# Attention scores in PSUM tiles of 1024 keys, with two tiles for transposed probabilities

## The chip, the cores and the metric

One core of one Trainium2 chip runs the kernel. The metric is the device time of one execution in microseconds (us), and the number compared is the median of a kernel's runs. Engines are named as the profile names them: PE multiplies matrices (PEld is its weight load, which overlaps PE), DVE is VectorE, ACT is ScalarE, POOL is GpSimd, SP issues DMAs. PE writes its results to PSUM, which has 8 banks of 2 KiB in each of 128 partitions; a bank holds 512 float32 values.

## What is computed

One layer of a decoder. A projection of the normalised input gives queries, keys, values, an indexer's queries and keys, gates, and the inputs of a gated MLP. The indexer chooses at most 256 causal keys for each of 2048 prompt queries; attention runs over the chosen keys only; the two halves are gated, joined, projected and added to the residual. 64 sample queries do the same against paged caches. Cut to the part in question:

```python
def sparse_attend(q, kg, vg, valid):          # 8 query heads x 64, 4 key heads
    s = jnp.einsum('btgrd,btkgd->btgrk', qg, kg) * HEAD_DIM ** -0.5
    s = jnp.where(valid[:, :, None, None, :], s, -jnp.inf)
    p = jax.nn.softmax(s, axis=-1).astype(vg.dtype)
    o = jnp.einsum('btgrk,btkgd->btgrd', p, vg)
```

The kernel doesn't gather: it computes all causal scores and adds a mask that the selection left in memory.

## The kernel before

Three phases follow each other. Phase A projects and selects. Phase B (`phase_b`) is the attention, and the change lies in it alone. Phase C is the output projection and the gate.

Phase B takes the prompt in 16 blocks `i` of 128 queries; block `i` sees `W = 128 * (i + 1)` keys. A block has four steps, one for each key head `g`, and a step has the two query heads `r` that share it. For each step two lists of units are made and interleaved by even spacing:

- `scores(i, g)`: for each head, chunks of 512 keys. A chunk is two matmuls into a PSUM tile `b_s` (a high and a low part of the queries, L1117 and L1118) and one DVE instruction (L1119) which adds the mask, writes the masked scores to `b_sm` in SBUF and keeps the running minimum in `b_st`; each chunk but the first takes the minimum of the one before as its start, and a short read of the accumulator follows each. After the last chunk ACT takes the exponential of the whole row in place (L1126).
- `values(i, g)` of the step before: pairs of key blocks. A pair is four PE transposes of probabilities into one PSUM tile `b_tp` (L1152), a split into `b_pt` by the helper at L126 and L127 (ACT copies the high part, then DVE subtracts it from the tile to get the low part, so the tile is held until DVE has read it), and, two pairs later, one matmul for each key block with the values into `b_o` (L1169). At the end of a step ACT and DVE add the two halves of `b_o` (L1185, L1186 to `b_x`), two PE transposes turn it (L1193), and POOL scales it.

Between units, `sample_attention` is drawn on as a filler: it transposes cache pages into `b_tp` tiles too (L1318, copied by ACT at L1320), takes `b_s` tiles for its scores (L1327, L1330) and `b_tp` tiles for its outputs (L1373). `prep_q` transposes the next block's queries through `b_tp` (L1050).

PSUM in phase B is four `b_tp` tiles of a bank, two `b_s` tiles of a bank and two `b_o` tiles of a bank, which is all eight. The pools hand tiles out in rotation, so a new tile waits for the last reader of the one that had its place. The program's scheduler decides the final order on each engine; each engine then runs its list in that order.

Of the kernel before, what the change touches and what calls it, by code (L numbers as in the profile page):

```python
# [9 lines left out]
F32 = mybir.dt.float32  # L10
# [7 lines left out]
PSUM = bass.MemoryType.PSUM  # L18
# [28 lines left out]
SPS = 0  # L47
SY = 8
X_POOL = 0
SPB = 2  # L50
# [63 lines left out]
class Builder:  # L114
# [961 lines left out]
    def phase_b(self, eb):  # L1076
        tc, nc, I, O = self.tc, self.nc, self.I, self.O
# [6 lines left out]
        with ExitStack() as es:  # L1084
            pool = lambda name, bufs, **kw: es.enter_context(tc.tile_pool(name=name, bufs=bufs, reuse_waits="tile", **kw))
# [1 line left out]
            smp = pool("b_sm", LAG_SM)  # L1087
            ptp = pool("b_pt", 2 + PV_LAG)
            wk = pool("b_wk", 2)
            tp = pool("b_tp", 6 - SPB - SPS, space=PSUM)  # L1090
            sps = pool("b_sps", SPS, space=PSUM) if SPS else tp
            sp = pool("b_s", SPB, space=PSUM)
            op = pool("b_o", 2, space=PSUM)
            Kst, Vst, ms, prs = self.Kst, self.Vst, self.ms, self.prs
# [3 lines left out]
            def scores(i, g, pr):  # L1098
                qh, ql, ga, stt = pr
                m = ms[i]  # L1100
                W = 128 * (i + 1)
                out, units = [], []
                for r in range(2):
                    h = 2 * g + r
                    if W > SEQ // 2:
                        sm = smp.tile([128, SEQ], F32, name="b_sm")[:, :W]
                    else:
                        if r == 0:
                            both = smp.tile([128, 2, SEQ // 2], F32, name="b_sm")
                        sm = both[:, r, :W]  # L1110
                    out.append(sm)

                    def chunk(c, h=h, sm=sm):
                        c0, cn = c * 512, min(512, W - c * 512)
                        ps = sp.tile([128, 512], F32, name="b_s")[:, :cn]
                        rhs = Kst[c][:, g, :cn]
                        nc.tensor.matmul(ps, lhsT=qh[:, h], rhs=rhs, start=True, stop=False)  # L1117
                        nc.tensor.matmul(ps, lhsT=ql[:, h], rhs=rhs, start=False, stop=True)  # L1118
                        V.tensor_tensor_reduce(out=sm[:, c0:c0 + cn], in0=ps, in1=m[:, c0:c0 + cn], scale=1.0,  # L1119
                                               scalar=3.0e38 if c == 0 else stt[:, h, c - 1:c], op0=OP.add, op1=OP.min,  # L1120
                                               accum_out=stt[:, h, c:c + 1])

                    def expo(e, h=h, sm=sm):
                        part = sm[:, e * EXP:min(W, e * EXP + EXP)]
                        c = -(-W // 512) - 1
                        nc.scalar.activation(part, part, AF.Exp, bias=stt[:, h, c:c + 1], scale=-1.0,  # L1126
                                             accum_out=stt[:, h, 4 + e:5 + e])
                        if e:
                            V.tensor_tensor(stt[:, h, 4:5], stt[:, h, 4:5], stt[:, h, 5:6], OP.add)

                    ne = -(-W // EXP)
                    units += [(lambda c=c, f=chunk: f(c)) for c in range(-(-W // 512) - 1)]
                    units += [lambda f=chunk, e=expo: (f(-(-W // 512) - 1), e(0))]
                    if ne > 1:
                        units += [lambda e=expo: e(1)]
                sms[i, g] = out
                return units
# [70 lines left out]
            sms, obs, tail = {}, {}, []  # L1208
            fill = self.sample_attention(sc, sp, sps)
            fill_n = 0.0  # L1210
            parts = lambda b: 2 * -(-(b + 1) // 4) + -(-(b + 1) // 2) + 1
            rate = FILL / (sum(4 * parts(b) for b in ORDER) - FILL_AT * parts(ORDER[0]))
            due = []
            for si in range(len(steps) + max(LAG, LAG_SMALL)):
                A, B = [], []
                if si < len(steps):
                    i, g = steps[si]
                    A = scores(i, g, prs[i])
                    at = si // 4
                    if g == 1 and at + 2 < NB:  # L1220
                        self.load_mask(ORDER[at + 2])
                    due.append((si + (LAG_SMALL if i < 7 else LAG), steps[si]))
# [28 lines left out]
    def sample_attention(self, c, sp, tp):  # L1251
        tc, nc, I, O = self.tc, self.nc, self.I, self.O
# [16 lines left out]
        ps = tp.tile([128, 2, 2, 128], F32, name="b_tp")  # L1269
# [10 lines left out]
        ps = tp.tile([128, 2, 2, 128], F32, name="b_tp")  # L1280
# [11 lines left out]
        def fetch():  # L1292
            if todo:
                s, ch = todo.pop(0)
                pg = c.tile([128, 2, 256], F32, name="s_pg", bufs=6)
                self.pages(pg.rearrange("p k d -> p (k d)"), "cache_k", s, ch, 2)
                pgs.append(pg)

        fetch()
        for hf in range(2):  # L1300
# [6 lines left out]
            for ch in range(5):  # L1307
                n = 256 if ch < 4 else 64
                kTs = {}
                for s4 in range(4):  # L1310
                    s = hf * 4 + s4
                    if ch < 4:
                        pg = pgs.pop(0)
                        fetch()
                        for p in range(2):
                            ps = tp.tile([128, 2, 2, 128], F32, name="b_tp").rearrange("p a b n -> p (a b n)")
                            for k in range(2):
                                nc.tensor.transpose(ps[:, k * 128:k * 128 + 128], pg[:, k, p * 128:p * 128 + 128], ident)  # L1318
                            kT = c.tile([128, 256], F32, name="s_kT", bufs=8)
                            nc.scalar.activation(kT.rearrange("d (x k) -> d x k", k=2), ps[:, :256].rearrange("d (k x) -> d x k", k=2), AF.Copy)  # L1320
                            kTs[s4, p] = kT
                            yield
                for p in range(2):
                    S = sp.tile([128, 512], F32, name="b_s")[:, :n]
                    for s4 in range(4):
                        kT = kTs[s4, p] if ch < 4 else knT[:, p]
                        nc.tensor.matmul(S[s4 * 32:s4 * 32 + 32], lhsT=QS[:, hf * 4 + s4, p].rearrange("p g r t -> p (g r t)"),  # L1327
                                         rhs=kT, start=True, stop=True, tile_position=(0, s4 * 32))
                    w = stt[:, hf * 2 + p]
                    V.tensor_tensor_reduce(out=SM[p][:, ch * 256:ch * 256 + n], in0=S,  # L1330
                                           in1=m[:, ch * 256:ch * 256 + n], scale=1.0,
                                           scalar=3.0e38 if ch == 0 else w[:, ch - 1:ch], op0=OP.add, op1=OP.min,
                                           accum_out=w[:, ch:ch + 1])
                    yield
# [16 lines left out]
            for kb in range(9):  # L1351
                kr = 128 if kb < 8 else 64
                ps = tp.tile([128, 2, 2, 128], F32, name="b_tp")
# [11 lines left out]
            for ch in range(5):  # L1365
                kbs = range(2 * ch, min(9, 2 * ch + 2))
                o = tp.tile([128, 2, 2, 128], F32, name="b_tp")
                for kb in kbs:
                    kr = 128 if kb < 8 else 64
                    for p in range(2):  # L1370
                        for s4 in range(4):
                            vt = vts[ch, s4][:, kb % 2] if kb < 8 else vn
                            nc.tensor.matmul(o[s4 * 32:s4 * 32 + 32, p, 0], lhsT=pts[kb][:kr, p, s4 * 32:s4 * 32 + 32],  # L1373
                                             rhs=vt[:kr, p * 128:p * 128 + 128], start=(kb == kbs[0] and p == 0),
                                             stop=(kb == kbs[-1]), tile_position=(0, s4 * 32), skip_group_check=True)
# [8 lines left out]
            ps = tp.tile([128, 2, 2, 128], F32, name="b_tp")  # L1384
# [9 lines left out]
        ps = tp.tile([128, 2, 2, 128], F32, name="b_tp")  # L1394
# [206 lines left out]
```

## Time and profile before

| | |
|---|---|
| median of 3 runs | 1873.06 us (1872.78 to 1878.46) |
| profiled execution: its own time | 1874.53 us |
| its span, first to last instruction | 1872.7 us |
| around the span | 1.8 us |
| phase B | 1026 to 1515 us, 489 us |
| busy over the span: PE, DVE, ACT, POOL | 97%, 66%, 54%, 32% |

Busy time is the union of instruction durations. PE's durations overlap, so its share alone doesn't tell how much room it has; the distance between the starts of neighbouring matmuls does. A chain of waits follows the last instruction back to what released it. Idle time on an engine that nobody waits for costs nothing.

### The profile page before, as it was taken

How to read it: one execution, taken by the hardware profiler on the slowest of the kernel's cores; microseconds unless marked ns; L12 is line 12 of the kernel's file. 1: busy time of each engine (PE TensorE's matmuls, PEld its weight loads, DVE VectorE, ACT ScalarE, POOL GpSimd, SP SyncE). 2: the span in 40 equal slices, each digit the busy share in tenths (PEclk: the TensorE clock that was granted, in tenths of full speed). 3: DMA queues.
4: the chain of work that ended last, by engine and by line, in shares of the span. 5: the costliest groups of instructions: out<-in, count | busy, mean ns of one | idle time of the engine just before them, and what ended most of it. 6: DMA issues, size and time to landing. Idle time of an engine off the chain costs nothing. (4 is left out here: it accounts for less than half of the span.)

```text
span 1872.7 us, 33926 instructions
## 1 busy us (share of the span) xinstructions
PE 1821.9 (97%) x11974; PEld 1599.1 (85%) x11974; DVE 1243.2 (66%) x3638; ACT 1019.7 (54%) x1912; POOL 608.2 (32%) x967
## 2 busy tenths in 40 slices
PE   7998999999999999999999899999999999999998
PEld 6997978999999999998988777788778878888887
DVE  4588753568788638768754788899979974233321
ACT  3234434446656636677665888688867753122121
POOL 4566362433013325004403642522234113222221
PEclk9998999999999999999999899999999999999999
DMA  8854665645445564454455551522133063223211
GB/s 241 283 182 145 212 204 188 212 126 157 127 154 167 201 185 144 142 169 154 151 195 169 144 138 49 157 63 72 54 87 116 12 226 109 75 96 107 93 37 46
DMA packets 243807, 261.54 MB, mean 140 GB/s; under 512 B 83177, under 2 KB 209841, under 8 KB 243249
## 3 DMA queue, kind: packets, MB, share of 16 engines
q1 hardware_dynamic: 147200, 144.10, 24.8%
q10 hardware_dynamic: 90544, 96.35, 15.8%
q0 software_dynamic: 5888, 18.88, 3.5%
q8 instruction: 95, 1.56, 0.3%
q14 instruction: 80, 0.65, 0.1%
HBM read 171.90 MB, written 87.37 MB: 138 GB/s over the span
## 5 line engine op out<-in xcount | busy, mean ns | idle before, releaser
L323 PE MATMUL z<-whi,hhi 128*128 128x256 f32 (+1 forms) x1792 | 463.4, 292 | 7.6 <-ACT qn L397 2.6
L324 PE MATMUL z<-wlo,hhi 128*128 128x256 f32 (+1 forms) x1792 | 454.4, 287 | 1.3 <-DVE wlo L293 1.3
L323 PEld LDWEIGHTS z<-whi,hhi 128*128 128x128 f32 x1792 | 342.1, 191 | 17.2 <-ACT qn L397 3.6
L324 PEld LDWEIGHTS z<-wlo,hhi 128*128 128x128 f32 x1792 | 342.4, 191 | 6.5 <-DVE wlo L293 1.5
L326 PE MATMUL z<-whi,hlo 128*128 128x256 f32 (+1 forms) x1792 | 262.1, 285 | 0.0
L326 PEld LDWEIGHTS z<-whi,hlo 128*128 128x128 f32 x1792 | 237.9, 189 | 2.2
L706 DVE SCALAR_TENSOR_TENSOR big<-dots,sgn,big 128x1024 f32<-128x1024 f32 (+7 forms) x176 | 179.0, 1017 | 48.2 <-ACT dots L704 43.1
L127 DVE TENSOR_TENSOR b_pt<-b_tp,b_pt 128x512 fp32r<-128x512 f32 (+1 forms) x288 | 183.3, 655 | 12.8 <-ACT b_pt L126 11.7
L1169 PE MATMUL b_o<-b_pt,Vst 128*128 128x512 f32 x544 | 184.0, 421 | 1.3 <-DVE b_pt L127 1.3
L704 ACT ACTIVATE dots<-dots 128x1024 f32<-128x1024 f32 (+7 forms) x176 | 139.7, 800 | 82.3 <-PE dots L702 78.5
L126 ACT ACTIVATE b_pt<-b_tp 128x512 fp32r<-128x512 f32 (+1 forms) x288 | 156.5, 579 | 43.2 <-PE b_tp L1152 39.3
L1152 PE MATMUL b_tp<-mats,b_sm 128*128 128x128 f32 x1088 | 170.8, 275 | 1.6 <-ACT b_sm L1126 0.7
L843 ACT ACTIVATE bfw<-big,tk 128x384 bf16<-128x384 f32 (+14 forms) x105 | 136.5, 1300 | 60.3 <-DVE tk L863 34.9
L1126 ACT ACTIVATE b_sm<-b_sm,b_st 128x128 f32<-128x128 f32 (+15 forms) x128 | 154.9, 1211 | 24.3 <-DVE b_st L1119 23.6
L1152 PEld LDWEIGHTS b_tp<-mats,b_sm 128*128 128x128 f32 x1088 | 132.3, 141 | 31.0 <-ACT b_sm L1126 3.3
L1117 PE MATMUL b_s<-Kst,b_qh 128*128 128x512 f32 (+3 forms) x320 | 138.3, 435 | 5.1 <-DVE b_st L1119 4.3
L1119 DVE CUSTOM_DVE_ANT_0 b_sm<-b_s,b_mask,b_st 128x512 f32<-128x512 f32 (+3 forms) x192 | 123.8, 645 | 18.4 <-PE b_s L1118 13.9
L701 PE MATMUL dots<-ki_stack,qih 128*128 128x512 f32 (+3 forms) x304 | 113.1, 373 | 3.4 <-DVE big L706 1.8
L1118 PE MATMUL b_s<-Kst,b_ql 128*128 128x512 f32 (+3 forms) x320 | 116.4, 368 | 0.0
L702 PE MATMUL dots<-ki_stack,qil 128*128 128x512 f32 (+3 forms) x304 | 109.4, 369 | 0.0
L1169 PEld LDWEIGHTS b_o<-b_pt,Vst 128*128 128x128 f32 x544 | 91.0, 190 | 20.9 <-DVE b_pt L127 5.5
L1484 PE MATMUL c_mm<-c_h_w_ple_gate,c_mh 128*128 128x512 f32 x272 | 108.8, 400 | 0.0
(349 smaller groups left out, 3742.7 us busy)
## 6 DMA issues: line engine op xcount, KB each, us to landing
whi<-s_wh ACTq DMA_DIRECT2D x52, 512.0 KB
wlo<-s_wl ACTq DMA_DIRECT2D x52, 512.0 KB
raw<-w_in SPq DMA_DIRECT2D x112, 128.0 KB
s_wh<-whi ACTq DMA_DIRECT2D x13, 1024.0 KB
s_wl<-wlo ACTq DMA_DIRECT2D x13, 1024.0 KB
s_r<-hlo SPq DMA_DIRECT2D x32, 256.0 KB
b_qr<-s_q SPq DMA_DIRECT2D x32, 256.0 KB
c_r<-s_r SPq DMA_DIRECT2D x16, 512.0 KB
```

What stands on the lines that cost most here:

```text
L126: nc.scalar.activation(hi, src, AF.Copy)
L127: nc.vector.tensor_tensor(lo, src, hi.bitcast(F32), OP.subtract)
L323: nc.tensor.matmul(z, lhsT=hh[:, k], rhs=wh[:, k, :n], start=(k == 0), stop=False)
L324: nc.tensor.matmul(z, lhsT=hh[:, k], rhs=wl[:, k, :n], start=False, stop=False)
L326: nc.tensor.matmul(z, lhsT=hl[:, k], rhs=wh[:, k, :n], start=False, stop=(k == 7))
L704: nc.scalar.activation(r, r, AF.Relu)
L706: nc.vector.scalar_tensor_tensor(a, r, self.sgn[:, b, h:h + 1], a, op0=OP.mult, op1=OP.add)
L843: nc.scalar.activation(junk, acc[:P], AF.Sign, bias=cur[:, 0:1], accum_out=cur[:, 1:2])
L1117: nc.tensor.matmul(ps, lhsT=qh[:, h], rhs=rhs, start=True, stop=False)
L1126: nc.scalar.activation(part, part, AF.Exp, bias=stt[:, h, c:c + 1], scale=-1.0, accum_out=stt[:, h, 4 + e:5 + e])
L1152: nc.tensor.transpose(ps[:, k, r], sm2[r][:, (k0 + k) * 128:(k0 + k) * 128 + 128], ident)
L1169: nc.tensor.matmul(o.rearrange("p a b -> p (a b)"), lhsT=Vst[:, kb, g].rearrange("p a d -> p (a d)"), rhs=pt[:, k].rearrange("p a b -> p ( ...
```

## The change

A score chunk becomes 1024 keys: its tile has two banks, it is filled by up to four matmuls of 512 keys (or two and a remainder), and one mask instruction with one accumulator read takes all of it. `b_s` keeps two tiles, which are now four banks, and `b_tp` goes from four tiles to two. The filler's pace is counted anew (`parts`), since a step has fewer units.

```diff
-            tp = pool("b_tp", 6 - SPB - SPS, space=PSUM)
+            tp = pool("b_tp", 6 - 2 * SPB - SPS, space=PSUM)
...
-                        c0, cn = c * 512, min(512, W - c * 512)
-                        ps = sp.tile([128, 512], F32, name="b_s")[:, :cn]
-                        rhs = Kst[c][:, g, :cn]
-                        nc.tensor.matmul(ps, lhsT=qh[:, h], rhs=rhs, start=True, stop=False)
-                        nc.tensor.matmul(ps, lhsT=ql[:, h], rhs=rhs, start=False, stop=True)
+                        c0, cn = c * 1024, min(1024, W - c * 1024)
+                        ps = sp.tile([128, 1024], F32, name="b_s")[:, :cn]
+                        for s0 in range(0, cn, 512):
+                            part(ps[:, s0:min(cn, s0 + 512)], (c0 + s0) // 512, h)
                         V.tensor_tensor_reduce(out=sm[:, c0:c0 + cn], in0=ps, in1=m[:, c0:c0 + cn], scale=1.0,
                                                scalar=3.0e38 if c == 0 else stt[:, h, c - 1:c], op0=OP.add, op1=OP.min,
                                                accum_out=stt[:, h, c:c + 1])
...
+                    def part(ps, c, h):
+                        rhs = Kst[c][:, g, :ps.shape[1]]
+                        nc.tensor.matmul(ps, lhsT=qh[:, h], rhs=rhs, start=True, stop=False)
+                        nc.tensor.matmul(ps, lhsT=ql[:, h], rhs=rhs, start=False, stop=True)
...
-                    units += [(lambda c=c, f=chunk: f(c)) for c in range(-(-W // 512) - 1)]
-                    units += [lambda f=chunk, e=expo: (f(-(-W // 512) - 1), e(0))]
+                    units += [(lambda c=c, f=chunk: f(c)) for c in range(-(-W // 1024) - 1)]
+                    units += [lambda f=chunk, e=expo: (f(-(-W // 1024) - 1), e(0))]
...
-            parts = lambda b: 2 * -(-(b + 1) // 4) + -(-(b + 1) // 2) + 1
+            parts = lambda b: 2 * -(-(b + 1) // 8) + -(-(b + 1) // 2) + 1
...
-                    S = sp.tile([128, 512], F32, name="b_s")[:, :n]
+                    S = sp.tile([128, 1024], F32, name="b_s")[:, :n]
```

In the changed code the score matmuls are L1124 and L1125, the mask L1118, the transposes L1156, the value matmuls L1173, the turning of `b_x` L1197.

PE in a step of block 15, before. `b_o<-mats,b_x` is the turning of the step before:

```order
L1152 MATMUL b_tp<-mats,b_sm 128x128 x12
L1117 MATMUL b_s<-Kst_12929,b_qh 128x512
L1118 MATMUL b_s<-Kst_12929,b_ql 128x512
L1193 MATMUL b_o<-mats,b_x 128x128 x2
L1117 MATMUL b_s<-Kst_12930,b_qh 128x512
L1118 MATMUL b_s<-Kst_12930,b_ql 128x512
L1169 MATMUL b_o<-b_pt,Vst 128x512 x2
L1152 MATMUL b_tp<-mats,b_sm 128x128 x4
L1169 MATMUL b_o<-b_pt,Vst 128x512 x2
L1152 MATMUL b_tp<-mats,b_sm 128x128 x4
```

PE at the same place of block 15, changed:

```order
L1197 MATMUL b_o<-mats,b_x 128x128 x2
L1124 MATMUL b_s<-Kst_12931,b_qh 128x512
L1125 MATMUL b_s<-Kst_12931,b_ql 128x512
L1124 MATMUL b_s<-Kst_12932,b_qh 128x512
L1125 MATMUL b_s<-Kst_12932,b_ql 128x512
L1156 MATMUL b_tp<-mats,b_sm 128x128 x4
L1173 MATMUL b_o<-b_pt,Vst 128x512 x2
L1156 MATMUL b_tp<-mats,b_sm 128x128 x4
L1173 MATMUL b_o<-b_pt,Vst 128x512 x2
L1156 MATMUL b_tp<-mats,b_sm 128x128 x4
L1173 MATMUL b_o<-b_pt,Vst 128x512 x2
L1156 MATMUL b_tp<-mats,b_sm 128x128 x4
```

The run of twelve transposes (three tiles) ahead of the scores is gone; the scores stand in groups of four matmuls, and from there to the end of the step groups of four transposes and two value matmuls alternate.

DVE in a step of block 15, before (`ISA` with two outputs is the mask, `ISA b_st` its accumulator read, `b_pt` the subtraction of the split):

```order
L1119 ISA b_sm,b_st<-b_s,b_mask,b_st 128x512
L1119 ISA b_st 128x1
L1199 RECIPROCAL b_st<-b_st 128x2
L1186 TENSOR_TENSOR b_x<-b_o,b_x 128x256
L1119 ISA b_sm,b_st<-b_s,b_mask,b_st 128x512
L1119 ISA b_st 128x1
L127 TENSOR_TENSOR b_pt<-b_tp,b_pt 128x2x256 x2
L1119 ISA b_sm,b_st<-b_s,b_mask 128x512
L1119 ISA b_st 128x1
L127 TENSOR_TENSOR b_pt<-b_tp,b_pt 128x2x256
```

DVE in a step of block 15, changed:

```order
L1118 ISA b_sm,b_st<-b_s,b_mask 128x1024
L1118 ISA b_st 128x1
L127 TENSOR_TENSOR b_pt<-b_tp,b_pt 128x2x256
L1118 ISA b_sm,b_st<-b_s,b_mask,b_st 128x1024
L1118 ISA b_st 128x1
L127 TENSOR_TENSOR b_pt<-b_tp,b_pt 128x2x256
L1118 ISA b_sm,b_st<-b_s,b_mask 128x1024
L1118 ISA b_st 128x1
L1190 TENSOR_TENSOR b_x<-b_o,b_x 128x256
L1118 ISA b_sm,b_st<-b_s,b_mask,b_st 128x1024
L1118 ISA b_st 128x1
L127 TENSOR_TENSOR b_pt<-b_tp,b_pt 128x2x256 x2
```

Eight masks of 512 in a step have become four of 1024, and they stand close together: four masks with two subtractions between them, then the other six subtractions.

## Rows read from the trace of the kernel before

**Rows 1.** The page: the chain that ended last, by engine, then by line.

```profile
PE 42%; DMA 1%; DVE 1%; ACT 1%; issue 0%; POOL 0%; DVEq 0%; ACTq 0%; SPq 0%; POOLq 0%
```

**Rows 2.** Stretches: length, busy us (instructions) of PE, PEld, DVE, ACT, POOL; clock, DMA.

```profile
1026.00:1515.00 489.00, 474.03 (x3156) 378.33 (x3155) 426.45 (x1169) 390.08 (x800) 163.95 (x269) 0.99 0.31 87
...
1039.00:1166.00 127.00, 122.71 (x823) 97.75 (x821) 109.53 (x332) 111.81 (x286) 56.18 (x105) 0.99 0.41 111
...
1267.00:1302.00 35.00, 35.00 (x226) 28.36 (x225) 32.16 (x84) 28.76 (x57) 9.08 (x16) 1.00 0.26 69
...
1441.00:1486.00 45.00, 44.97 (x267) 36.84 (x266) 42.95 (x110) 35.98 (x58) 5.30 (x13) 1.00 0.04 13
```

**Rows 3.** Start of a DVE step mark, `b_x`: two blocks, four steps each.

```profile
1267.84 0.42 DVE L1186 TENSOR_TENSOR b_x<-b_o,b_x 128x256 f32<-128x256 f32 x1
...
1302.16 0.42 DVE L1186 TENSOR_TENSOR b_x<-b_o,b_x 128x256 f32<-128x256 f32 x1
...
1441.12 0.40 DVE L1186 TENSOR_TENSOR b_x<-b_o,b_x 128x256 f32<-128x256 f32 x1
...
1485.82 0.41 DVE L1186 TENSOR_TENSOR b_x<-b_o,b_x 128x256 f32<-128x256 f32 x1
```

**Rows 4.** Timeline: start, duration, instruction. Scores on PE, then transposes of block 15.

```profile
1268.54 0.40 PE L1117 MATMUL b_s<-Kst,b_qh 128*128 128x512 f32 x1
...
1268.78 0.39 PE L1118 MATMUL b_s<-Kst,b_ql 128*128 128x512 f32 x1
...
1485.46 1.47 PE L1152 MATMUL b_tp<-mats,b_sm 128*128 128x128 f32 x12
```

**Rows 5.** The chain in order of time, end of phase B: start, length, piece.

```profile
1507.40 0.56 PE b_tp L1152 x3
...
1508.04 0.61 ACT b_pt L126
...
1508.67 0.70 DVE b_pt L127
...
1509.42 0.73 PE b_o L1169 x2
1510.15 0.44 PE b_tp L1152 x4
1510.58 0.46 PE b_o L1169 x2
```

**Rows 6.** Timeline of DVE and ACT, a step of block 15.

```profile
1488.01 0.68 DVE L1119 CUSTOM_DVE_ANT_0 b_sm<-b_s,b_mask 128x512 f32<-128x512 f32 x1
...
1488.62 0.69 DVE L127 TENSOR_TENSOR b_pt<-b_tp,b_pt 128x512 fp32r<-128x512 f32 x1
1489.22 0.74 DVE L1119 CUSTOM_DVE_ANT_0 b_sm<-b_s,b_mask,b_st 128x512 f32<-128x512 f32 x1
1489.88 0.08 DVE L1119 DVE_READ_ACCUMULATOR2_ANT b_st<- 128x1 f32 x1
...
1486.05 1.58 ACT L126 ACTIVATE b_pt<-b_tp 128x512 fp32r<-128x512 f32 x3 [0.92 <-PE b_tp L1152]
```

**Rows 7.** Groups by shape, 1026 to 1515 us: count, busy us, mean ns, idle before.

```profile
L1119 DVE CUSTOM_DVE_ANT_0 b_sm<-b_s,b_mask,b_st 128x512 f32<-128x512 f32 x120 | 89.5, 746 | 15.2 <-PE b_s L1118 11.9
...
L1126 ACT ACTIVATE b_sm<-b_sm,b_st 128x2048 f32<-128x2048 f32 x8 | 16.1, 2011 | 3.4 <-DVE b_st L1119 3.1
...
L1126 ACT ACTIVATE b_sm<-b_sm,b_st 128x1408 f32<-128x1408 f32 x8 | 11.8, 1470 | 2.5 <-DVE b_st L1119 2.5
```

**Rows 8.** Groups by shape, whole span: phase A's widest DVE read of PSUM.

```profile
L706 DVE SCALAR_TENSOR_TENSOR big<-dots,sgn,big 128x1024 f32<-128x1024 f32 x80 | 102.3, 1279 | 22.0 <-ACT dots L704 17.4 <-POOL big L674 3.7
...
L706 DVE SCALAR_TENSOR_TENSOR big<-dots,sgn,big 128x512 f32<-128x512 f32 x16 | 11.9, 742 | 1.0 <-ACT dots L704 0.9
```

**Rows 9.** Groups by shape, 1268 to 1302 us: the filler's page copies.

```profile
L1320 ACT ACTIVATE s_kT<-b_tp 128x256 f32<-128x256 f32 x8 | 3.1, 386 | 1.4 <-PE b_tp L1318 1.4
```

**Rows 10.** Waits of PEld in phase B: us in total, times, longest.

```profile
PEld b_s L1117 <- DVE b_st L1119: 11.1, 21, 2.6
```

More of the change, by code (lines that the diff above doesn't have):

```diff
@@ L1121, in chunk @@
                                                accum_out=stt[:, h, c:c + 1])
+                    def part(ps, c, h):
+                        rhs = Kst[c][:, g, :ps.shape[1]]
+                        nc.tensor.matmul(ps, lhsT=qh[:, h], rhs=rhs, start=True, stop=False)
+                        nc.tensor.matmul(ps, lhsT=ql[:, h], rhs=rhs, start=False, stop=True)
                     def expo(e, h=h, sm=sm):
                         part = sm[:, e * EXP:min(W, e * EXP + EXP)]
-                        c = -(-W // 512) - 1
+                        c = -(-W // 1024) - 1
                         nc.scalar.activation(part, part, AF.Exp, bias=stt[:, h, c:c + 1], scale=-1.0,
```

## The prediction

> **What bounds the kernel now.** I read the page's chain first: PE holds 42% of the span in the part that the chain reaches back over, and no other engine holds more than 1% [rows 1]. That part is phase B and what follows. Next come the stretches: over phase B PE is busy 474 of 489 us, DVE 426, ACT 390 [rows 2]. PE's busy time flatters it, because matmul durations overlap, so I went to the distances between starts. Two neighbouring score matmuls of 512 columns start 0.24 us apart [rows 4]; twelve transposes take 1.47 us with a last one of 0.27, so 0.11 each [rows 4]; four transposes and two value matmuls alternate at 0.44 and 0.46 [rows 5]. A step of block 15 has 8 pairs, 16 score matmuls and two turning transposes: 8 × 0.90 + 16 × 0.235 + 0.22 = 11.2 us of PE. Between the step marks four steps took 1485.82 - 1441.12 = 44.7 us, 11.2 each [rows 3]. PE is full there. Block 10 took 34.3 us for four steps, 8.6 each [rows 3], with PE busy for all 35.0 us of the stretch [rows 2]. DVE is nearly full too: 42.95 of 45 us late, 32.2 of 35 in the middle [rows 2]. So in the long blocks PE sets the time, with DVE some 5 to 8% behind, and what keeps PE full is that transposes can run ahead into four tiles.
>
> **What the change takes away.** A head of W keys needs W/512 masks now and W/1024 then, both rounded up: over 16 blocks and 8 heads 320 become 192. On DVE a first mask of 512 is followed 0.61 us later by the next instruction, a later one, with its accumulator read, 0.66 us later [rows 6]. No mask of 1024 is in the trace; the nearest is phase A's read of PSUM, 742 ns at 512 and 1279 at 1024, against 746 for a mask of 512 [rows 7, 8]: 0.54 us for 512 more elements. So a mask of 1024 costs 0.61 + 0.54 = 1.15 us as a first one, 1.20 later, and each merging saves 0.66 - 0.54 = 0.12 us of DVE. The bounds are no saving (twice 0.66) and the whole 0.66. I take 0.12, since the width rows have the same engine, source and type. 128 × 0.12 = 15 us of DVE are freed. No PE, ACT or DMA work goes. PE waits for the score tile 21 times, 11.1 us in all [rows 10]; a part of that goes as well.
>
> **What it adds: a ring of two tiles.** This is the term that decides. A transposed pair keeps its tile from its first transpose until DVE has subtracted. Where nothing is in the way that is three transposes to their end and the hand-over 0.64, ACT 0.63, DVE 0.75 until PE goes on, and 0.11 for the fourth transpose: 2.1 us [rows 5]. Four tiles allow a pair every 0.53 us, two allow one every 1.06, and PE needs 0.90 for a pair alone [rows 5]. So in the groups of "four transposes, two value matmuls" that now fill the end of a step, the ring is slower than PE even when both other engines are idle. They are not: ACT's exponential is 2.01 us in block 15 and 1.47 in block 10 [rows 7], during which no tile is copied, and the masks stand close together on DVE, 1.15 to 1.20 us each, with a subtraction queued behind each. Before, the run of twelve transposes covered just that place.
>
> I walked one step of block 15 through the three lists as the changed program has them, with PE at 0.44 (pair), 0.47 (two value matmuls), 0.94 (scores of 1024); ACT 0.49 a copy, which is (1.58 - 0.61)/2 [rows 6], ready after 0.60; DVE 0.60 a subtraction [rows 6], ready after 0.70. Number the pairs in PE's order; the masks are A to D. DVE has A, sub 7, B, sub 8, C, `b_x`, D, subs 1 to 6. PE has pair 8, scores C, pair 1, scores D, pair 2, scores A', turning, scores B', pairs 3 to 7, with value matmuls between; a pair waits for the subtraction of the pair two before, scores for the mask two before. From the start of A: A ends at 1.15, sub 7 at 1.8, B at 3.0, sub 8 at 3.6, C at 4.7, D at 6.2. Scores C start at 1.25 instead of 0.55, since A has to leave the tile first; pair 1 is at 2.7, scores D 3.1, pair 2 4.0, scores A' 4.95, scores B' 6.3. ACT takes the first exponential at 3.2, copies 1 and 2 after 5.2, the second exponential at 6.6, copy 3 not before 8.6. So sub 3 ends at 9.9 and pair 5, which needs its tile, starts there, 0.9 us after PE was free. Pairs 6 and 7 follow at the ring's pace, at 10.9 and 11.9, sub 6 is done at 12.7, and with it the next A starts. The step takes **12.7 us against 11.2: 1.5 us more**, all of it PE waiting for tiles.
>
> The same walk in block 10 (5.5 pairs, masks of 1024 and 384) adds the filler: a page transposed into a `b_tp` tile waits for ACT alone, 0.39 us, two to a step [rows 9]. But its copy stands behind an exponential, and with two tiles the pair two places on waits for it. There the waits are 0.4 before the scores, 1.0 for a copy behind the second exponential, 0.7 behind the next copies, and short ones; I get 11.4 us with three pages in the step, about 11.1 with two: **2.5 us more than 8.6**. Here the cover is the four tiles, and nothing takes its place.
>
> **The sum.** Blocks 8 to 11, 16 steps at 2.5: 40 us. Blocks 12 to 15, 16 steps at 1.5: 24 us. Blocks 0 to 7, 32 steps with one to four pairs, weren't walked; the first seven of them take 127 us, with DVE busy 110 and ACT 112 [rows 2], so there is more room to wait in and fewer pairs to lose: I take half of the late price, 0.8 us a step, 26 us. Together 90 us. The freed 15 us of DVE are in the walks already. The profiled execution took 1874.53 us, of which 1.8 lie around the span; 90 more are 1964.5, and the median is 1.5 below that execution: **1963 us**. From below the ring's price is nothing, if ACT and DVE always reach a tile in time, and the masks' gain stays; from above it is the block 10 price in all 64 steps, 160 us, which gives 2033. I take a value nearer the upper end because the two walked rows of steps are half of all steps and the longer half.
>
> On the small edits: the two-bank score tile lets PE run 1024 keys ahead of DVE, which is in the walk; the filler's new pace moves pages between units and removes none; the first scores of block 0 go behind the last key preparation, a few matmuls of 0.24 us [rows 4], which I cost at nothing, since PE's starting stretch has idle time beside it, and at 2 us if it hasn't.
>
> **A rule to weigh.** The rows show a DVE that is 87% busy over phase B and 95% late, with PE full beside it [rows 2]. The Trainium skill, "Perfetto Trace Analysis", section "Optimizing Scalar/DVE Operations", gives both answers: larger operations raise throughput if the engine is saturated, and if Scalar or Vector aren't saturated but cause bubbles on other engines, breaking instructions up may let work finish sooner. It puts the overhead of a DVE instruction on PSUM at about 125 ns, an estimate of 16 us for 128 fewer, close to the 15 from the rows. By the first half the change should win; by the second it should lose. I hold DVE to be the unsaturated case, since PE is the full one.
>
> **Rivals.** First, the masks decide (faster). If DVE is what really paces phase B, and PE only follows it, then 15 us come off and the ring hardly binds, because DVE reaches its subtractions sooner: 1873 - 15 = 1858. For it speaks DVE's 95% late [rows 2] and the 11.1 us that PE waits for score tiles [rows 10]; against it the chain [rows 1] and the block 15 step that equals PE's own work. It decides if tiles are mostly free when PE wants them, that is if ACT's copy comes within 0.1 us. This is the case which the rule's first half gives.
>
> Second, the ring binds only where the walk is surest, in the 16 steps of blocks 12 to 15, and elsewhere the filler's units give ACT and DVE time to catch up: 24 us, 1897. For it speaks that blocks 0 to 7 have slack; against it that the filler takes tiles itself.
>
> Third, ring and masks cancel, 15 against 15: 1873. Fourth, the block 10 price everywhere, 2033; against it speaks that short blocks have few pairs. That the change doesn't do what it says is no rival: the program has 192 masks of up to 1024 and two tiles.
>
> **Chances.** The forecast (1905 to 2020) 0.73, the second rival 0.10, the first 0.10, cancelling 0.03, the fourth 0.04. The range 1885 to 2020 holds the forecast and nearly all of the second rival, 0.82. About 0.3% is what a measurement of this kernel can tell from no change. Faster by more than that: 0.10; within it: 0.03; slower: 0.87.
>
> **What would show it.** In the profile after: masks x192, DVE's busy time in phase B about 15 us less; phase B near 580 us; PE's busy share in it down from 97% to the high eighties; new waits of PEld or PE at the transposes on DVE's `b_pt` and ACT's `b_pt` of tens of us; ACT's waits for transposes grown; step marks some 12.7 us apart in block 15 and 11 in block 10. Phases A and C unchanged. I am wrong if step marks in block 15 are 11.2 us apart or less, or if the lost time stands at the score matmuls waiting for masks rather than at transposes waiting for tiles.

## The result, and the profile after

The changed kernel takes 1972.45 us (median of 4 runs, 1969.36 to 1976.3) against 1873.0 before: ratio 1.0523, 95% interval 1.0508 to 1.0537. It is 99 us slower; 1963 was forecast. The profiled execution took 1969.36 us, with a span of 1967.6 us.

The chain on the page, by engine, answers to [rows 1]:

```profile
PE 24%; ACT 3%; DVE 2%; issue 1%; DMA 1%; POOL 0%; SPq 0%; DVEq 0%; ACTq 0%; POOLq 0%
```

The chain followed one queue for 42% before; now it reaches back a shorter way and goes through ACT and DVE as well. Phase B in one stretch (length, then busy us of PE, PEld, DVE, ACT, POOL) answers to the first of [rows 2]:

```profile
1026.00:1609.00 583.00, 520.44 (x3152) 376.56 (x3150) 414.88 (x911) 400.56 (x797) 163.60 (x269) 0.99 0.26 73
```

Phase B grew from 489 to 583 us, nearly all of the loss, at a granted clock of 0.99 of full speed in both. PE's busy share fell from 97% to 89%: its idle time grew from 15 to 63 us, and the other 46 us of the loss lie in its busy time, a union of overlapping durations, for as many matmuls. DVE is busy 12 us less than the 426 of before, and no engine has taken the place of the bound: all are idler. What they wait for stands in the waits of phase B (us in total, times, longest):

```profile
ACT b_pt L126 <- PE b_tp L1156: 99.4, 144, 4.1
DVE b_pt L127 <- ACT b_pt L126: 69.8, 114, 4.2
...
PEld b_tp L1156 <- DVE b_pt L127: 38.6, 61, 1.6
...
PEld b_s L1124 <- DVE b_st L1118: 21.4, 46, 1.5
...
PE b_tp L1156 <- DVE b_pt L127: 19.1, 30, 1.5
```

It is a circle: ACT waits for transposes, DVE for ACT's copy, and the transposes for DVE's subtraction, which frees the tile. PEld's wait at the score matmuls, 11.1 us before [rows 10], didn't shrink but doubled. PE in a step of block 15 (start, duration, instruction) shows the place:

```profile
1566.67 0.60 PE L1156 MATMUL b_tp<-mats,b_sm 128*128 128x128 f32 x4
1567.03 0.71 PE L1173 MATMUL b_o<-b_pt,Vst 128*128 128x512 f32 x2
1567.57 0.60 PE L1156 MATMUL b_tp<-mats,b_sm 128*128 128x128 f32 x4
1567.93 0.70 PE L1173 MATMUL b_o<-b_pt,Vst 128*128 128x512 f32 x2
1569.39 0.66 PE L1156 MATMUL b_tp<-mats,b_sm 128*128 128x128 f32 x4 [0.76 <-DVE b_pt L127]
```

After the scores two pairs go at PE's pace, 0.90 us apart, since both tiles are free; the third is due at 1568.5 and begins at 1569.39, when DVE has freed the first pair's tile. What made that late stands on ACT, then on DVE:

```profile
1566.04 2.00 ACT L1130 ACTIVATE b_sm<-b_sm,b_st 128x2048 f32<-128x2048 f32 x1
...
1568.03 1.07 ACT L126 ACTIVATE b_pt<-b_tp 128x512 fp32r<-128x512 f32 x2
...
1568.64 1.29 DVE L127 TENSOR_TENSOR b_pt<-b_tp,b_pt 128x512 fp32r<-128x512 f32 x2 [0.32 <-ACT b_pt L126]
```

The first pair was transposed by 1567.27, but ACT was in the exponential of a row and took up the copy at 1568.03, 0.76 us later; PE's idle time is the same 0.76. It is no exception. PE itself waited 26 us in phase B for tiles that the subtraction freed (the 19.1 us above and smaller waits), and for 19 of these 26 us the copy had come behind an exponential, without a pause of ACT between.

The step marks of DVE answer to [rows 3]. A mark closes the values of a step, so the stretch from 1441.12 to 1485.82 before, and this one after, closes the last three steps of block 14 and the first of block 15:

```profile
1524.23 0.42 DVE L1190 TENSOR_TENSOR b_x<-b_o,b_x 128x256 f32<-128x256 f32 x1
...
1536.68 0.42 DVE L1190 TENSOR_TENSOR b_x<-b_o,b_x 128x256 f32<-128x256 f32 x1
...
1551.30 0.42 DVE L1190 TENSOR_TENSOR b_x<-b_o,b_x 128x256 f32<-128x256 f32 x1
...
1563.97 0.42 DVE L1190 TENSOR_TENSOR b_x<-b_o,b_x 128x256 f32<-128x256 f32 x1
...
1576.90 0.42 DVE L1190 TENSOR_TENSOR b_x<-b_o,b_x 128x256 f32<-128x256 f32 x1
```

The four steps take 12.5, 14.6, 12.7 and 12.9 us, 13.2 in the mean, where 11.2 was before and 12.7 was walked. The marks that answer to block 10's:

```profile
1320.22 0.42 DVE L1190 TENSOR_TENSOR b_x<-b_o,b_x 128x256 f32<-128x256 f32 x1
...
1367.08 0.42 DVE L1190 TENSOR_TENSOR b_x<-b_o,b_x 128x256 f32<-128x256 f32 x1
```

Four steps in 46.9 us, 11.7 each, against 8.6 before and 11.1 walked.

### The profile page after: what moved, and what is told of

It reads as the page before. It is cut to its first block, busy times and chain, and to the rows that moved or that the text cites. A ratio compares the mean times of both kernels' runs of the same rounds, so it can differ in the third digit from the quotient of the medians.

```text
span 1967.6 us, 33570 instructions
## 1 busy us (share of the span) xinstructions
PE 1866.8 (95%) x11974; PEld 1596.5 (81%) x11974; DVE 1231.3 (63%) x3382; ACT 1032.2 (52%) x1912; POOL 604.7 (31%) x967
## 5 line engine op out<-in xcount | busy, mean ns | idle before, releaser
L126 ACT ACTIVATE b_pt<-b_tp 128x512 fp32r<-128x512 f32 (+1 forms) x288 | 161.9, 572 | 102.3 <-PE b_tp L1156 99.4
L1173 PE MATMUL b_o<-b_pt,Vst 128*128 128x512 f32 x544 | 193.6, 437 | 4.9 <-DVE b_pt L127 3.4
L1156 PE MATMUL b_tp<-mats,b_sm 128*128 128x128 f32 x1088 | 171.8, 280 | 22.2 <-DVE b_pt L127 19.1
L1156 PEld LDWEIGHTS b_tp<-mats,b_sm 128*128 128x128 f32 x1088 | 127.2, 141 | 73.4 <-DVE b_pt L127 38.6
L1124 PE MATMUL b_s<-Kst,b_qh 128*128 128x512 f32 (+3 forms) x320 | 127.7, 405 | 14.6 <-DVE b_st L1118 10.3
L1118 DVE CUSTOM_DVE_ANT_0 b_sm<-b_s,b_mask 128x1024 f32<-128x1024 f32 (+5 forms) x112 | 119.7, 1074 | 15.8 <-PE b_tp L1156 8.2
L1125 PE MATMUL b_s<-Kst,b_ql 128*128 128x512 f32 (+3 forms) x320 | 114.8, 371 | 0.0
L1489 PE MATMUL c_mm<-c_l_w_ple_gate,c_mh 128*128 128x512 f32 x272 | 106.7, 392 | 0.0
```

The lines of the kernel that those rows point to most:

```text
L126: nc.scalar.activation(hi, src, AF.Copy)
L1156: nc.tensor.transpose(ps[:, k, r], sm2[r][:, (k0 + k) * 128:(k0 + k) * 128 + 128], ident)
L1173: nc.tensor.matmul(o.rearrange("p a b -> p (a b)"), lhsT=Vst[:, kb, g].rearrange("p a d -> p (a d)"), rhs=pt[:, k].rearrange("p a b -> p ( ...
L1489: nc.tensor.matmul(z, lhsT=hi[:, k], rhs=wts[k][1][:, ns], start=False, stop=(b == SB and k == nk - 1))
```

## The experiments

The theory: a ring of two tiles, each held from its first transpose until DVE has read it, is what costs; the wide masks are worth next to nothing. The rivals: long masks standing close together delay the subtractions; ACT's exponentials do; or taking tiles away costs by something other than their rate. Each kernel is compared with the kernel before on the same chip (medians there 1872.75 to 1875.48 us), and ratios are to that.

**Two tiles alone.**

```diff
-            tp = pool("b_tp", 6 - SPB - SPS, space=PSUM)
+            tp = pool("b_tp", 2, space=PSUM)
```

> The kernel before with two b_tp tiles in place of four and nothing else (two banks stay unused; masks of 512, b_s tiles of one bank). If the ring of two tiles is what costs, nearly the whole loss is here: 1950 to 2000 us, with waits of PEld at the transposes on DVE's b_pt as in the changed kernel (some 38 us or more). If instead the long masks or their standing close together cost the time, and the ring costs little, it stays near the kernel before: 1873 to 1890 us.

Measured: 1955.97 us, ratio 1.0446 (1.0428 to 1.0465): 83 of the 99 us, without a wide mask or a wide tile. Among its waits in phase B are the four of the changed kernel:

```profile
ACT b_pt L126 <- PE b_tp L1152: 93.7, 128, 2.4
...
DVE b_pt L127 <- ACT b_pt L126: 47.8, 88, 2.4
PEld b_s L1117 <- DVE b_st L1119: 27.9, 71, 1.0
PEld b_tp L1152 <- DVE b_pt L127: 26.1, 46, 1.7
```

PEld's wait at the transposes came out as 26 us where 38 were expected; the time is within the range for the ring, and the rival that asked for 1873 to 1890 us is out.

**Three tiles.** The same line with 3.

> The kernel before with three b_tp tiles. A tile's shortest life is 2.1 us, so three allow a pair every 0.70 us, less than PE's 0.90: the ring theory expects a wait only where ACT or DVE comes late, 10 to 35 us, 1883 to 1908 us. If two tiles cost by something else than their rate (a different order of the program), the cost should grow evenly with each tile taken, half of that of two tiles: about 1915 to 1925 us.

Measured: 1889.78 us, ratio 1.0087 (1.0067 to 1.0107), 17 us. The price is not even by tile: the step from four to three costs 17, the next one 66. That is the shape of a rate: 0.70 us for a pair with three, under PE's 0.90, 1.06 with two; the 17 us that are left were forecast as waits where ACT or DVE comes late; they weren't followed in the trace. One thing wasn't held fixed here or below: the scheduler makes a new order for each kernel.

**A tile that is free sooner.** With two tiles, ACT copies the whole tile to SBUF, POOL makes the high part from the copy, DVE the low part:

```diff
+                    pf = ptp.tile([128, 2, 2, 128], F32, name="b_pf", bufs=3)[:, :kn]
+                    nc.scalar.activation(pf, ps[:, :kn], AF.Copy)
+                    nc.gpsimd.tensor_scalar(pt[:, :kn, 0:2], pf, 1.0, 1.0, op0=OP.mult, op1=OP.mult)
+                    V.tensor_tensor(pt[:, :kn, 2:4], pf, pt[:, :kn, 0:2].bitcast(F32), OP.subtract)
```

> The kernel before with two b_tp tiles, but ACT copies the whole tile to SBUF in float32 (three buffers), POOL makes the high part from the copy and DVE the low part, so a tile is free after ACT: its shortest life falls from 2.1 to about 1.4 us, a pair every 0.70 us, the rate of three tiles with the old life (b_x is cut to the half that is used and b_mix to one buffer, for room). If a tile's life in the ring is the price, it comes near three tiles: 1885 to 1920 us. If the price is something else that comes with two tiles, it stays within 15 us of 1956.

Measured: 1941.76 us, ratio 1.0362 (1.0344 to 1.0381). That missed the range for the ring and lies 14 us under 1956, just inside the mark for "something else". Yet the wait at the transposes is down, from 26.1 us to 9.5, and a new one at the value matmuls is the largest of PE's:

```profile
PEld b_o L1166 <- DVE b_pt L1158: 45.5, 95, 2.1
...
PEld b_tp L1152 <- ACT b_pf L1156: 9.5, 26, 1.8
```

So the control is needed to read it.

> Control: the same split by ACT, POOL and DVE with four b_tp tiles. It tells what the longer way to b_pt costs by itself: 1870 to 1885 us if POOL keeps up (its part is some 0.6 us a pair against 0.9 for PE), more than 1900 if POOL's copy or the room for it holds PE up.

Measured: 1930.39 us, ratio 1.0293 (1.0276 to 1.0311), the upper of the two cases: the longer way costs 55 us with a full ring. But from four tiles to two the loss is now 11 us (1930.39 to 1941.76), where the old split lost 83. Together with the shorter wait at the transposes this speaks for the time that a tile is held as the price. It isn't a clean measure: both kernels are held up elsewhere, and while PE waits for `b_pt`, tiles have time to come free. Where the 55 us go shows in the control's phase B, as in [rows 2], and its groups (count, busy us, mean ns, idle before):

```profile
1026.00:1566.00 540.00, 505.21 (x3148) 376.30 (x3148) 474.70 (x1167) 390.08 (x797) 393.44 (x557) 0.98 0.28 82
```

```profile
L1158 DVE TENSOR_TENSOR b_pt<-b_pf,b_pt 128x512 fp32r<-128x512 f32 x256 | 221.7, 881 | 18.6 <-POOL b_pt L1157 17.2 <-issue 1.0
L1157 POOL TENSOR_SCALAR b_pt<-b_pf 128x512 fp32r<-128x512 f32 x256 | 187.0, 743 | 45.7 <-ACT b_pf L1156 39.8 <-PE b_o L1166 2.1 <-PE b_s L1118 1.7
...
L1156 ACT ACTIVATE b_pf<-b_tp 128x512 f32<-128x512 f32 x256 | 146.1, 602 | 73.5 <-DVE b_pt L1158 45.2 <-PE b_tp L1152 15.4 <-PE b_o L1190 4.0
```

DVE is busy 475 us where 426 were before [rows 2], because its subtraction has grown longer, and phase B has grown by about as much, from 489 to 540. The three steps of a copy's life are 0.60, 0.74 and 0.88 us, 2.2 in all; three buffers allow a pair every 0.74 us, so the rate alone would leave room beside PE's 0.90. ACT waits 45.2 us for DVE to give a copy's buffer back all the same, since DVE comes late to its subtractions, and the value matmuls stand behind them too. This is a new wait, in SBUF, and not the one under test.

**Wide tiles with short masks.** The changed kernel with two masks of 512 for each tile:

```diff
+                        for s0 in range(0, cn, 512):
+                            e0, en, k = c0 + s0, min(512, cn - s0), (c0 + s0) // 512
+                            V.tensor_tensor_reduce(out=sm[:, e0:e0 + en], in0=ps[:, s0:s0 + en], in1=m[:, e0:e0 + en], scale=1.0,
+                                                   scalar=3.0e38 if k == 0 else stt[:, h, k - 1:k], op0=OP.add, op1=OP.min,
+                                                   accum_out=stt[:, h, k:k + 1])
```

> The changed kernel with two masks of 512 for each tile of 1024: 320 masks again, tiles and ring as in the changed kernel. Ring theory: the masks' 15 us of DVE are worth little or nothing where tiles are waited for, so 1965 to 1990 us. If long masks that keep subtractions waiting are the cause, the shorter ones give back a good part: below 1930 us.

Measured: 1965.14 us, ratio 1.0497 (1.0477 to 1.0516), beside 1.0523 (1.0508 to 1.0537) for the changed kernel. The intervals touch. So with this ring merging the masks gains nothing and may cost a few us, and long masks aren't the cause.

**Wide tiles with a full ring.** The changed kernel with `SPB = 1`: one wide score tile, four `b_tp`.

> The changed kernel with one b_s tile of two banks in place of two, and so four b_tp tiles: wide masks, a full ring. Ring theory: the waits at the transposes go, and what is left is PE waiting for the only score tile, at most a mask of 1.2 us for some of the 192 chunks: 1870 to 1940 us. If wide masks cost the time, it stays at 1960 us or more.

Measured: 1926.67 us, ratio 1.0282 (1.0261 to 1.0302). It is 46 us faster than the changed kernel with the same masks, but no gain over the kernel before. Two of its waits:

```profile
PEld b_s L1124 <- DVE b_st L1118: 25.5, 46, 3.9
PEld b_tp L1156 <- ACT b_sm L1130: 24.0, 42, 1.3
```

The score matmuls now wait for the only tile, and the transposes for the exponential of a row whose scores came late. Half of what the ring lost is lost there instead.

**Wide tiles with a ring of three**, paid for by one `b_o` tile in place of two, and its control with narrow tiles:

> The changed kernel with one b_o tile in place of two, and so three b_tp tiles: wide masks, two wide score tiles, a ring of three. Ring theory: the ring of three costs 17 us with narrow masks, so this comes near the next kernel, within 15 us of it either way, and far below 1972: 1885 to 1925 us. If wide tiles are what cost, it stays within 25 us of the changed kernel.

> Its control: the kernel before with one b_o tile and three b_tp tiles, masks of 512. If the second b_o tile is spare, 1885 to 1895 us as with three tiles and two b_o; if steps collide on the only b_o tile (the turning at its end takes some 2 us before the next step's first value matmul), 64 steps lose up to 1 us each: 1900 to 1955 us.

Measured: 1932.49 us (1.0317, 1.03 to 1.0334) wide, 1911.74 us (1.0211, 1.0194 to 1.0229) narrow. The wide one missed both marks: it lies 40 us under the changed kernel, more than the rival allowed, and 21 over its control, more than the theory did. The second `b_o` tile isn't spare: with three tiles it is worth 22 us (1889.78 against 1911.74). And with ring and `b_o` alike, wide tiles cost 21 us more than narrow ones.

**More score tiles of the old width.** The kernel before with `SPB = 4`, so four narrow `b_s` and two `b_tp`: the changed kernel's PSUM, the old chunks.

> The kernel before with four b_s tiles of 512 and two b_tp tiles: the changed kernel's division of PSUM, with the old chunks. If what the changed kernel loses beyond two tiles (16 us) is the wide chunk, this lies at the two-tile kernel's 1956 us or up to 10 below it, for the two more score tiles; if it comes of the scores running further ahead of the values, it lies at 1965 to 1975.

Measured: 1980.22 us, ratio 1.0558 (1.0541 to 1.0576), above both marks. By the ratios, since the chips differ, that is 21 us more than two score tiles with the same ring. So it isn't the width, nor the filler's new pace, which this kernel doesn't have: room for twice as many scores costs some 20 us. The pair with three tiles above, where width and room changed together, shows the same 21. Its waits, up to 1600 us of a phase that ends at 1615, beside those of the two-tile kernel:

```profile
DVE b_pt L127 <- ACT b_pt L126: 65.0, 100, 2.3
PEld b_tp L1152 <- DVE b_pt L127: 40.6, 53, 1.9
...
PEld b_s L1117 <- DVE b_st L1119: 18.2, 50, 1.0
```

PE waits less for score tiles (18.2 for 27.9) and more for transposed ones (40.6 for 26.1). The scheduler had also placed the scores earlier in the lists, and the two weren't taken apart.

**Shorter exponentials.** `EXP = 1024` in place of 2048, with two tiles and, as a control, with four:

> The kernel before with two b_tp tiles and the exponential of a row in two pieces of up to 1024 (blocks 8 to 15). With two tiles a copy behind an exponential of 1.5 to 2.0 us leaves PE without a tile; if that is a large part of the price, shorter pieces give back 10 to 30 us of the 83: 1925 to 1945 us. If the ring's own pace of 1.06 us for a pair is most of it, it stays within 10 us of 1956.

> Control of the short exponential: the kernel before with rows exponentiated in two pieces and four b_tp tiles. If the pieces cost 13 us by themselves (64 more instructions on ACT and as many accumulator reads and small DVE sums), 1880 to 1890 us; if they are free here, 1870 to 1876, and with two tiles shorter pieces do harm.

Measured: 1968.65 us (1.0513, 1.0496 to 1.0531) with two, 1879.77 us (1.002, 1.001 to 1.0029) with four. Short pieces cost some 4 us with a full ring, just under the first mark, and 13 with two tiles, above both marks; they give nothing back. But they didn't shorten the time for which ACT is taken. With two tiles, in 58 of the 64 rows that have two pieces, the second follows the first at once:

```profile
1554.38 1.14 ACT L1126 ACTIVATE b_sm<-b_sm,b_st 128x1024 f32<-128x1024 f32 x1
...
1555.52 1.14 ACT L1126 ACTIVATE b_sm<-b_sm,b_st 128x1024 f32<-128x1024 f32 x1
...
1556.65 0.36 ACT L1196 ACTIVATE b_mix<-b_o 128x256 f32<-128x256 f32 x1
```

That keeps ACT for 2.27 us, where the single exponential above kept it for 1.99. So the rival of the exponentials isn't out: a longer hold cost 13 us with two tiles and 4 with four, which rather speaks for it, and no run let a copy in between the halves.

**Five tiles**, with one `b_o`:

> The kernel before with one b_o tile and five b_tp tiles. The ring's price fell from 83 us (two) to 17 (three) to nothing known (four): a fifth tile should bring 0 to 10 us, less what the missing b_o tile costs: 1865 to 1900 us. A clear gain would say that four tiles still hold PE up.

Measured: 1908.61 us, ratio 1.0198 (1.0181 to 1.0215), above the range, and within 4 us of three tiles with one `b_o`. Past three the ring has nothing left to give there; the missing `b_o` sets the time. No kernel here beats the one before.

## Why the prediction was right

**The bound.** PE was full, and freeing DVE didn't shorten it in any kernel here: the 12 us that DVE lost in phase B (15 were expected) came back nowhere, and wide tiles cost 21 us at a ring of three. What wide masks would give beside a full ring and two score tiles isn't shown; that would take ten banks. The first rival, 1858 us, stood on DVE being the pace, and is out. How near DVE is to that place the control of the early copy shows: 48 us more of DVE made phase B 51 us longer. Of the rule from the Trainium skill, "Perfetto Trace Analysis", section "Optimizing Scalar/DVE Operations", the first half (larger operations can help a saturated engine) isn't borne out with a ring of two: one mask or two for a tile made no difference beyond the noise (1.0523 and 1.0497), with DVE busy 71% of phase B; beside a DVE that is 95% busy it wasn't tried alone. The second half, that breaking them up may help, isn't shown: shorter masks gave nothing beyond the noise, and the shorter exponentials, which ran without a pause, cost time.

**The mask's size.** Of the 72 first masks of 1024 and the 8 chained ones:

```profile
L1118 DVE CUSTOM_DVE_ANT_0 b_sm<-b_s,b_mask 128x1024 f32<-128x1024 f32 x72 | 87.5, 1217 | 11.5 <-PE b_tp L1156 7.9 <-PE b_s L1125 1.7 <-POOL b_ga L1206 1.0
...
L1118 DVE CUSTOM_DVE_ANT_0 b_sm<-b_s,b_mask,b_st 128x1024 f32<-128x1024 f32 x8 | 10.2, 1274 | 0.0
```

1274 ns chained; 746 and the 537 of phase A's rows gave 1283.

**The ring.** The step that decided held: 83 of 99 us come with two tiles alone, 17 with three, and 11, with the reserve above, where a tile is freed by ACT. The walk of block 15 was right in its mechanism: ACT runs as walked, an exponential, two copies, an exponential, two copies; the third pair starts 0.92 us after it was due (0.76 of it idle) where 0.9 was walked, and the next two follow 0.96 and 1.11 us apart, walked at 1.0. In length the walk gave 12.7, and the four steps of the stretch have a mean of 13.2. The 11.2 us beside which it was set aren't block 15's alone, since half of the stretch's scores are block 14's:

```profile
L1126 ACT ACTIVATE b_sm<-b_sm,b_st 128x2048 f32<-128x2048 f32 x4 | 8.0, 2012 | 1.9 <-DVE b_st L1119 1.8
L1126 ACT ACTIVATE b_sm<-b_sm,b_st 128x1920 f32<-128x1920 f32 x4 | 7.6, 1901 | 1.9 <-DVE b_st L1119 1.9
```

Taken over the same marks, the loss is 2.0 us a step where 1.5 was walked. Block 10 was walked at 11.1 and took 11.7, a loss of 3.1 a step for 2.5.

**The sum.** It came out 9 us low. Half of that is the offset at its end: the median was put 1.5 us below the profiled execution and lies 3.1 above it. The rest comes of terms that miss in both directions. Step marks at the borders of the block groups, before and then after:

```profile
1203.27 0.41 DVE L1186 TENSOR_TENSOR b_x<-b_o,b_x 128x256 f32<-128x256 f32 x1
...
1342.54 0.42 DVE L1186 TENSOR_TENSOR b_x<-b_o,b_x 128x256 f32<-128x256 f32 x1
...
1392.29 0.42 DVE L1186 TENSOR_TENSOR b_x<-b_o,b_x 128x256 f32<-128x256 f32 x1
```

```profile
1241.07 0.42 DVE L1190 TENSOR_TENSOR b_x<-b_o,b_x 128x256 f32<-128x256 f32 x1
...
1414.09 0.42 DVE L1190 TENSOR_TENSOR b_x<-b_o,b_x 128x256 f32<-128x256 f32 x1
...
1474.31 0.42 DVE L1190 TENSOR_TENSOR b_x<-b_o,b_x 128x256 f32<-128x256 f32 x1
```

With two tiles alone:

```profile
1230.18 0.41 DVE L1186 TENSOR_TENSOR b_x<-b_o,b_x 128x256 f32<-128x256 f32 x1
```

Block 8 begins at 1203.27 before and 1241.07 after, and the first step mark lies 3 us earlier after, so the unwalked blocks 0 to 7 lost 41 us where 26 were put, 1.3 a step and not 0.8. With two tiles alone block 8 begins at 1230.18, 27 us later than before, so some 11 of the 16 us that the changed kernel loses beyond the ring fall in these blocks too. They have short steps, but blocks 0 to 5 draw the filler at double pace, whose pages pass through the same two tiles; that this is the reason isn't shown. PE's largest waits there are 4.5 us for cache pages and 3.6 for the score tile, and the one at the pairs' transposes is 2.7. From 1241.07 to 1414.09 blocks 8 to 11 take 173.0 us, before, from 1203.27 to 1342.54, 139.3: 34 lost where 40 were put. Blocks 12 to 15 lost 22, where 24 were put, and that this term fits is partly luck: one by one the four lost 10.5, 1.1, 8.0 and 2.2 us. The filler's last output matmuls end at 1401 us before, in the second of them, and at 1467 after, in the first, which moves some of the time.

**What failed.** The two-bank score tile was taken as harmless room to run ahead ("in the walk"): room for twice the scores costs some 20 us by itself, which the walk, being made on the changed lists, held without naming. A part of the 11.1 us that PEld waits for a score tile was to go; it became 21.4. And half of the late price for blocks 0 to 7 was an estimate that no row carried: 1.3 us a step, not 0.8. What stays open is how much of the ring's price the exponentials make: the trace shows copies behind them where PE waits, and no run took them away.

## What to carry to other kernels

Count a rotating PSUM tile's life, first write to last read over all engines that it passes, and divide by the number of tiles: if that exceeds the work of the engine that fills it, that engine waits, however idle the others are. Here 1.06 us against 0.90 cost 83 us. The division is a lower bound: 0.70 against 0.90 still cost 17, and a reader that comes late lengthens the life, as ACT does behind the exponential above. Saving instructions on an engine that isn't the bound was worth nothing here, and paying for it in tiles on the path cost. When the last reader is what holds a tile, reading it out sooner can take the wait away from the ring, but then the copy's buffers wait for the same late reader, and its work may grow. To learn what a long instruction costs that others stand behind, look in the trace whether the shorter pieces let anything in between.

## What the runs showed beside

With four tiles and the early copy, DVE's subtraction of 128x512 took 881 ns in the mean, its sources in SBUF and POOL at work beside it, where the same subtraction out of PSUM has a mean of 687 ns in the changed kernel:

```profile
L127 DVE TENSOR_TENSOR b_pt<-b_tp,b_pt 128x512 fp32r<-128x512 f32 x256 | 173.7, 687 | 69.2 <-ACT b_pt L126 67.0
```

The trace tells what does it. Two subtractions from SBUF, the first during a run of three POOL instructions, the second with POOL idle:

```profile
1517.41 2.21 POOL L1157 TENSOR_SCALAR b_pt<-b_pf 128x512 fp32r<-128x512 f32 x3 [0.26 <-ACT b_pf L1156]
...
1518.07 1.09 DVE L1158 TENSOR_TENSOR b_pt<-b_pf,b_pt 128x512 fp32r<-128x512 f32 x1 [0.57 <-POOL b_pt L1157]
...
1527.87 0.68 DVE L1158 TENSOR_TENSOR b_pt<-b_pf,b_pt 128x512 fp32r<-128x512 f32 x1
```

Of the 256, the 53 with no POOL instruction beside them have a mean of 682 ns, and the 128 with one for over 70% of their time 986. In the changed kernel, where one source is in PSUM, the 31 with POOL beside them for over 70% of their time stay at 687. So it takes both, two sources in SBUF and POOL at work, and that is where the control's longer DVE time comes from.
